# Weight matmuls in runs of one width: hi and lo parts grouped per half block, in a two-layer encoder

## The chip, the cores and the metric

The kernel runs on one core of one Trainium2 chip. The metric is device time in microseconds. The kernel before has a median of 2025.33 us over three runs (2021.2 to 2026.46).

## The reference

What is computed is a two-layer encoder for 256 tokens of width 2048, all in float32:

```python
for l in range(DEPTH):                       # 2 layers
    h = rms_norm(x, norm1_g[l])
    q, k, v, gu, gv = jnp.split(h @ w_in[l], splits, axis=-1)
    ...                                      # windowed attention of 8 heads; spatial gating in chunks of 128
    mixed = jnp.concatenate([rms_norm(attn, attn_out_g[l]), rms_norm(sgu, sgu_out_g[l])], axis=-1)
    x = x + mixed @ w_o[l]
    x = x + conv_gated_ffn(rms_norm(x, norm2_g[l]), w_up[l], conv_w[l], conv_b[l], w_down[l])
```

`conv_gated_ffn` multiplies by `w_up` (2048 x 11264), runs a three-tap convolution over the tokens, gates with silu, and multiplies by `w_down` (5632 x 2048). Nearly all work is in these weight matmuls.

## The kernel before

**Exact parts.** TensorE takes the operands as `fp32r`, a rounded float32. Each weight and each activation is therefore kept as two parts, hi (the rounded value) and lo (the rest), and a product is hi·hi + hi·lo + lo·hi. `split_weights` loads a megabyte of weights into a `raw` tile (L92, SyncE's queue, SP), makes `hi` tiles of 1024 columns on ScalarE (L102) and `lo` tiles on VectorE (L103). There are 3 `raw` buffers and 4 each of `hi` and `lo`. All this is traced as urgent, so the scheduler puts it as early as buffers allow.

**Token-major projections** (`rows_by_cols`, L117 to L119): the activations are the stationary operand, 512 columns of weights stream past, and three 512-wide matmuls in turn make the three products. They compute q, k, v and half of the gating input, at the start of each layer.

**Feature-major projections** (`unit`): 128 x 128 weights are the stationary operand and the 256 tokens stream past. An activation tile holds hi and lo of all tokens side by side (2 x 256 columns). So a hi weight meets all 512 columns (L136, both parts at once), and a lo weight meets the 256 hi columns (L137). One unit makes 256 output features in two PSUM banks, one for each half `i`; it walks over K in blocks of up to 8 groups of 128 rows (`UB`), and each block is one call of `split_weights`: two hi tiles and two lo tiles. `unit` does the gating half of the input projection (w_gu, 4 units in each layer), the output projection (w_o, 8), the up projection (w_up, 44), and the down projection in two parts (w_down, 8 units with 24 groups of K and 8 with 20). That is 2496 hi and 2496 lo matmuls in each layer. `joined` and `residual` then take the result from PSUM.

**Order.** The Tile framework's scheduler sets each engine's order from the traced program, its priorities and the buffers. Within a block, `unit` lists (k, i) with k outside; the unit's last block is sorted so that half 0 is complete before half 1. For each (k, i), hi and lo matmul follow each other.

The lines of attention that come up below: L170 to L172 are the three products of small attention matmuls, L204 broadcasts a per-token factor with the help of ones.

Of the kernel before, what the change touches and what calls it, by code (L numbers as in the profile page):

```python
# [14 lines left out]
P = 128  # L15
D = 2048
SEQ = 256
DEPTH = 2
DFF = 5632
HD = 128  # L20
# [6 lines left out]
KB = 4  # L27
UW = 256
UB = 8
AHEAD = 100000  # L30

# columns of a layer's per-feature parameters, features on partitions
C_N1, C_AG, C_SG, C_N2, C_CW = 0, 16, 24, 32, 48
N_COL = 48 + 4 * 2 * NF
# a layer's row parameters, to be broadcast over partitions
R_QG, R_KG, R_SINK, R_LG, R_LB, R_BS = 0, 128, 256, 264, 264 + 1024, 264 + 2048


# [1 line left out]
def encoder(ctx: ExitStack, tc: tile.TileContext, xT, w_in, w_gu, w_o, w_up, w_down, wsT, pcol, prow, rope, out):  # L40
    nc = tc.nc
# [29 lines left out]
    def mm():  # L71
        return mmp.tile([P, 2, W], F32, tag="mm", name="mm")
# [10 lines left out]
    def urgent():  # L83
        return tc.high_priority(offset=AHEAD)

    # ---- weights: hi and lo parts that add up to the float32 value exactly
    def split_weights(src, step=2 * W):
        n = src.shape[-1]
        with urgent():
            raw = rawp.tile([P, 4 * W], F32, tag="raw", name="raw")  # L90
            if step == 2 * W:
                nc.sync.dma_start(raw[:, :n], src)  # L92
            his, los = [], []
            for h in range(0, n, 2 * W):
                hi = hip.tile([P, 2 * W], F32R, tag="hi", name="hi")
                lo = lop.tile([P, 2 * W], F32R, tag="lo", name="lo")
                for a in range(0, 2 * W, step):
                    part = raw[:, h + a : h + a + step]
                    if step < 2 * W:
                        nc.sync.dma_start(part, src[:, h + a : h + a + step])  # L100
                    cs = slice(a, a + step)
                    nc.scalar.activation(hi[:, cs], part, AF.Copy)  # L102
                    nc.vector.tensor_tensor(out=lo[:, cs], in0=part, in1=hi[:, cs].bitcast(F32), op=ALU.subtract)  # L103
                his.append(hi)
                los.append(lo)
        return his, los

    # tokens x columns: ps[:, m, :] += act(k)[:, m].T @ w(k)
    def rows_by_cols(ps, acts, src, first, last, step=2 * W):
        his, los = split_weights(src, step)  # L110
        for kk in range(KB):
# [6 lines left out]
                nc.tensor.matmul(ps[:, m, :], acts[kk][:, 0, ms], wl, start=False, stop=False)  # L118
                nc.tensor.matmul(ps[:, m, :], acts[kk][:, 1, ms], wh, start=False, stop=s1)  # L119

    # columns x tokens, in two halves: [w.T @ hi + wl.T @ hi | w.T @ lo]
    def unit(acts, w, ps=None, k0=0, k1=None, first=True, last=True):
        ps = mm() if ps is None else ps
        bank = [ps[:, i, :] for i in range(2)] if not isinstance(ps, list) else ps
        k1 = len(acts) if k1 is None else k1
        for b in range(k0, k1, UB):
            n = min(UB, k1 - b)
            his, los = split_weights(w[:, b * UW : (b + n) * UW])
            order = [(k, i) for k in range(b, b + n) for i in range(2)]
            if last and b + n == k1:  # L130
                order.sort(key=lambda v: v[1])
            for k, i in order:
                c = (k - b) % KB * UW + i * P
                wh, wl = (t[(k - b) // KB][:, c : c + P] for t in (his, los))
                s0, s1 = first and k == k0, last and k == k1 - 1
                nc.tensor.matmul(bank[i], wh, acts[k].rearrange("p a b -> p (a b)"), start=s0, stop=False)  # L136
                nc.tensor.matmul(bank[i][:, :SEQ], wl, acts[k][:, 0, :], start=False, stop=s1)  # L137
        return ps

    def joined(ps):  # L140
# [24 lines left out]
        nc.vector.tensor_tensor(out=lo, in0=src, in1=hi.bitcast(F32), op=ALU.subtract)  # L165
        return hi, lo

    # out (+)= a.T @ b from parts
    def matmul3(out, a, b, start=True, stop=True):
        nc.tensor.matmul(out, a[0], b[0], start=start, stop=False)  # L170
        nc.tensor.matmul(out, a[0], b[1], start=False, stop=False)  # L171
        nc.tensor.matmul(out, a[1], b[0], start=False, stop=stop)  # L172

    # squares of feature-major rows, added up block by block
    def add_squares(acc, src, first):
        if first:
            nc.scalar.activation(acc, src, AF.Square)
# [9 lines left out]
        nc.gpsimd.tensor_tensor(out=r, in0=v, in1=mhalf[:, :width], op=ALU.pow)  # L187
        return r

    # 1/rms of every token, tokens on partitions, from squares with features on partitions  # L190
    def inv_rms_cols(acc, n, tag):
        t = tp([P, 2])
        nc.vector.tensor_tensor(out=acc[:, 0, :], in0=acc[:, 0, :], in1=acc[:, 1, :], op=ALU.add)
# [1 line left out]
            nc.tensor.matmul(t[:, m : m + 1], acc[:, 0, m * P : (m + 1) * P], ones[:, :1], start=True, stop=True)  # L195
        return inv_rms(t, n, tag, 2)

    # the same with tokens along the free dimension, on all partitions
    def as_rows(r):
        t = tp([P, SEQ])  # L200
        for m in range(2):
# [4 lines left out]
        nc.scalar.copy(rb, t)  # L206
        return rb

    # ---- loads that every layer needs
    def layer_params(l, eng):  # L210
        pc = lay.tile([P, N_COL], F32, tag="pc", name="pc")
        eng.dma_start(pc[:, :C_CW], pcol[l, :, :C_CW])
        return pc
# [34 lines left out]
                rows.append(t)  # L248
        return ws, rows

    # rotated rows (times the norm's gain): nh heads of [P, nh * HD]
    def rotate(rows, m, nh, tab):
        v = rows.rearrange("p (h d) -> p h d", d=HD)
        a = sl([P, nh, HD])
# [16 lines left out]
        nc.scalar.activation(sq, rows, AF.Square)  # L271
        nc.vector.tensor_reduce(out=ms, in_=sq.rearrange("p (h d) -> p h d", d=HD), axis=AX.X, op=ALU.add)

    # one group's heads, in steps to be traced between the projections' blocks
    def attend(g, ps, r, kT, v, tab, qk, nsink, acc, outs):
        ms = st([P, 2, 4], "qms")
        rot = []
# [74 lines left out]
            outs.append(o)  # L352
        yield

    # feature-major rows times gain and 1/rms, in parts
    def normed(tiles, g0, pc, rb):
        got = []
        for j, t in enumerate(tiles):
# [6 lines left out]
                got.append(split_plain(n))  # L365
        return got

    # ---- start
    with urgent():
        pc = layer_params(0, nc.sync)  # L370
    qk = None
# [1 line left out]
    make_identity(nc, ident)  # L373
    mask = const.tile([P, 2, SEQ], F32, tag="mask", name="mask")
    nc.gpsimd.memset(mask, 0.0)
    # token p sees key 128 + j when j <= p; token 128 + p sees key j when j >= p
    nc.gpsimd.affine_select(
        out=mask[:, 0, P:], in_=mask[:, 0, P:], compare_op=ALU.is_ge, fill=MASKED,
        base=0, pattern=[[-1, P]], channel_multiplier=1,
# [2 lines left out]
        out=mask[:, 1, :P], in_=mask[:, 1, :P], compare_op=ALU.is_ge, fill=MASKED,  # L382
# [25 lines left out]
    for l in range(DEPTH):  # L408
        pc, qk = params
        acts = hT  # L410

        def in_rows(ps, c, b):
            # the very first block comes in smaller pieces
            step = W if (l, c, b) == (0, 2, 0) else 2 * W
            src = w_in[l, c, :, b * KB * W : (b + 1) * KB * W]
            rows_by_cols(ps, acts[b * KB : b * KB + KB], src, b == 0, b == NB - 1, step)

        # keys and values, and the first queries
        psk, psq = mm(), mm()
        for b in range(NB):  # L420
            if l == 0:
# [18 lines left out]
        for m in range(2):  # L440
            t = sl([P, W])
# [6 lines left out]
        for m in range(2):  # L448
            a = rotate(kv[m][:, : 2 * HD], m, 2, tabs[1])
            nc.vector.tensor_tensor(  # L450
                out=a, in0=a, in1=rk[:, 2 * m : 2 * m + 2].unsqueeze(2).to_broadcast([P, 2, HD]), op=ALU.mult
# [21 lines left out]
            it = attend(g, ps, r1, kT, vs, tabs[0], qk, nsink, acca, att)  # L473
            return lambda: next(it)

        # second queries, the first group's attention between them
        first = group_steps(0, psq)
        first()
        ps = chunk(1, [[], [], [turned_keys], [first]])
        second = group_steps(1, ps)  # L480
        second()

        # gates of the spatial part
        vn = []
        stats = st([P, 2, 2, 6], "bns")
        for i in range(2):
            ps = chunk(3 + i, [[[first], [first, second], [first], [second]], [[], [second], [], [second]]][i])
            for m in range(2):
                t = row("vn")
# [43 lines left out]
        for i in range(2):  # L533
            for m in range(2):
                t = vn[2 * i + m]
# [20 lines left out]
        gated(3)  # L556
        gate(3)

        # output projection: the attention half of K first, while the gating half ends
        hT = []  # L560
        accx = lay.tile([P, 2, SEQ], F32, tag="acc", name="acc")
        with urgent():
# [3 lines left out]
        for u in range(8):  # L566
            if u < 3:
                ps = unit(mixT, w_o[l, u], pre[u], NK // 2, NK, first=False)
            else:
                ps = unit(mixT, w_o[l, u])  # L570
# [8 lines left out]
            pc1 = layer_params(l + 1, nc.sync)  # L579
            params = (pc1, layer_params_rest(l + 1, pc1, nc.sync))  # L580

        # gated convolution, features on partitions
        def convolved(ps, ch):
            s = joined(ps)
            nc.vector.tensor_tensor(out=s, in0=s, in1=r2b2[0], op=ALU.mult)  # L585
# [12 lines left out]
        for f0, f1 in ((0, 24), (24, NF)):  # L598
            ys = []
            for f in range(f0, f1, 2):  # L600
                y = sl([P, 2, SEQ])
                ps = unit(acts2, w_up[l, f // 2])
                if f == 0:
                    r2 = inv_rms_cols(accx, D, "y")
                    ps2 = unit(acts2, w_up[l, NF // 2])
                    r2b2.append(as_rows(r2).unsqueeze(1).to_broadcast([P, 2, SEQ]))
                nc.scalar.activation(y, convolved(ps, f), AF.Silu)
                t = convolved(unit(acts2, w_up[l, (NF + f) // 2]) if f else ps2, NF + f)
                nc.vector.tensor_tensor(out=y, in0=y, in1=t, op=ALU.mult)  # L609
                for i in range(2):  # L610
                    ys.append(split_plain(y[:, i, :]))

            # down projection of these features
            last = f1 == NF
            if last and more:
                hT = []
                accx = lay.tile([P, 2, SEQ], F32, tag="acc", name="acc")
            for u in range(8):
                ps = [tp([P, W]) for _ in range(2)] if last and not more and u == 7 else mm()
                unit(ys, w_down[l, u, :, f0 * UW : f1 * UW], ps)  # L620
                if last and not more:
                    for i in range(2):
                        part = ps[i] if isinstance(ps, list) else ps[:, i, :]
                        for a in (0, SEQ):
                            nc.vector.tensor_tensor(out=xs[u][:, i, :], in0=part[:, a : a + SEQ], in1=xs[u][:, i, :], op=ALU.add)
                        nc.sync.dma_start(out[:, 2 * u + i, :], xs[u][:, i, :])
                else:
                    residual(ps, u)
                if last and more:
                    next_rows(u, C_N1, params[0])  # L630
                    add_squares(accx, xs[u], u == 0)
# [56 lines left out]
```

## Time and profile before

| what | us |
|---|---|
| median of 3 runs | 2025.33 (2021.2 to 2026.46) |
| the profiled execution: first to last instruction | 2049.1 |
| TensorE busy (share of the span) | 2036.3 (99%) |
| weight loads busy | 1755.1 (86%) |
| VectorE busy | 1429.4 (70%) |
| ScalarE busy | 1076.5 (53%) |
| weights and the rest moved | 380.26 MB, 186 GB/s |

The profiled execution's own time is known only by its span; what lies around the span is not recorded for it. The table's engine rows are shares of an execution in which engines overlap. Matmuls are pipelined: the record of one reaches into the next, so that a busy TensorE isn't one at its peak, and pace is read from the distance of starts. In the rows that the prediction quotes, "L136 PE MATMUL ... x146: 391/391/391, 229.7 to 280.0" means 146 matmuls of line 136 with their least, median and greatest recorded duration in ns, and the starts of the first and the last in us. A row of the timeline begins with its start and its duration in us. A row of waits reads: who, for whom, us in total, times, longest.

### The profile page before, as it was taken

Reading aid. Unit: us, or ns where it says so; the run is one execution under the profiler, and the core shown is the slowest. Engines: PE = TensorE matmul, PEld = TensorE weight load, DVE = VectorE, ACT = ScalarE, POOL = GpSimd, SP = SyncE. Lnnn points to the kernel's source line nnn. Section 1 sums busy time; section 2 is a strip of 40 time slices with the busy share of each in tenths; the row PEclk is TensorE's granted clock in tenths of the full one; section 3 lists DMA queues with packets and bytes.
Section 4 is the critical chain, followed back from the end, with each engine's and each line's share of the span. In section 5 each row is a group of like instructions: output and inputs, shape, how many; then the busy total and the mean of one; then the engine's idle time right before and its main releaser. Section 6 shows DMA issues by size and latency. Waiting matters only on the chain.

```text
span 2049.1 us, 28253 instructions
## 1 busy us (share of the span) xinstructions
PE 2036.3 (99%) x11320; PEld 1755.1 (86%) x11320; DVE 1429.4 (70%) x1983; ACT 1076.5 (53%) x1427; POOL 19.5 (1%) x25
## 2 busy tenths in 40 slices
PE   8999999999999999999999999999999999999999
PEld 6888888888888888888888888888888888888887
DVE  6878767777745577776567887677777556777754
ACT  6575556555533455554445655555555334555532
POOL 0100000000000000000000000000000000000000
PEclk9999999999999999999999999999999999999999
DMA  8544555555555555555565445555555555555563
GB/s 294 203 149 156 185 190 185 187 188 188 189 186 185 185 185 185 185 186 175 197 224 183 146 147 189 183 189 188 189 187 188 186 185 185 185 185 185 182 209 124
DMA packets 59316, 380.26 MB, mean 186 GB/s; under 512 B 6832, under 2 KB 9648, under 8 KB 15280
## 3 DMA queue, kind: packets, MB, share of 16 engines
q1 hardware_dynamic: 59184, 378.46, 54.9%
q8 instruction: 88, 1.44, 0.3%
q14 instruction: 44, 0.36, 0.1%
HBM read 376.33 MB, written 2.10 MB: 185 GB/s over the span
## 4 chain that ended last, share of the span: by engine, by line
PE 96%; DVE 2%; ACT 0%; DMA 0%; issue 0%; POOL 0%; SPq 0%; ACTq 0%; POOLq 0%
PE mm L136 55%; PE mm L137 28%; PE mm L118 3%; PE mm L119 3%; PE mm L117 3%; DVE lo L103 1%; PE tp L136 0%; DMA raw<-in_w_in 0%; PE tp L342 0%; PE tp L170 0%; PE tp L518 0%; PE tp L172 0%; PE tp L171 0%; ACT hi L102 0%; PE tp L204 0%
## 5 line engine op out<-in xcount | busy, mean ns | idle before, releaser
L136 PE MATMUL mm<-sl,hi 128*128 128x512 f32 x4952 | 1748.6, 398 | 0.0
L137 PE MATMUL mm<-sl,lo 128*128 128x256 f32 x4952 | 1391.0, 281 | 0.0
L103 DVE TENSOR_TENSOR lo<-raw,hi 128x1024 fp32r<-128x1024 f32 (+1 forms) x706 | 861.6, 1221 | 547.5 <-ACT hi L102 542.1
L102 ACT ACTIVATE hi<-raw 128x1024 fp32r<-128x1024 f32 (+1 forms) x706 | 747.7, 1059 | 820.8 <-PE mm L136 626.6
L136 PEld LDWEIGHTS mm<-sl,hi 128*128 128x128 f32 x4952 | 930.1, 188 | 228.4
L137 PEld LDWEIGHTS mm<-sl,lo 128*128 128x128 f32 x4952 | 935.4, 189 | 0.7 <-DVE lo L103 0.3
L117 PE MATMUL mm<-hi,sl 128*128 128x512 f32 x320 | 126.8, 396 | 5.8 <-ACT hi L102 5.8
L118 PE MATMUL mm<-lo,sl 128*128 128x512 f32 x320 | 126.4, 395 | 0.8 <-DVE lo L103 0.8
L119 PE MATMUL mm<-hi,sl 128*128 128x512 f32 x320 | 125.8, 393 | 0.0
L589 ACT ACTIVATE sc<-ev,pc 128x256 f32<-128x256 f32 x176 | 95.2, 590 | 0.2
L593 DVE SCALAR_TENSOR_TENSOR sc<-ev,pc,sc 128x255 f32<-128x255 f32 x176 | 77.1, 479 | 0.1
L590 DVE SCALAR_TENSOR_TENSOR sc<-ev,pc,sc 128x255 f32<-128x255 f32 x176 | 77.0, 478 | 0.0
L117 PEld LDWEIGHTS mm<-hi,sl 128*128 128x128 f32 x320 | 60.7, 190 | 18.3 <-ACT hi L102 6.3
L118 PEld LDWEIGHTS mm<-lo,sl 128*128 128x128 f32 x320 | 60.7, 190 | 13.4 <-DVE lo L103 1.5
L119 PEld LDWEIGHTS mm<-hi,sl 128*128 128x128 f32 x320 | 60.7, 190 | 12.3
L158 ACT ACTIVATE sl<-sl 128x256 fp32r<-128x256 f32 x88 | 32.0, 411 | 72.0 <-DVE sl L609 72.0
L145 DVE TENSOR_TENSOR ev<-mm,ev 128x512 f32<-128x512 f32 x96 | 65.6, 684 | 0.1
L585 DVE TENSOR_TENSOR ev<-ev,rb 128x512 f32<-128x512 f32 x88 | 60.8, 692 | 2.8
L405 DVE TENSOR_TENSOR xs<-mm,xs 128x512 f32<-128x512 f32 x80 | 54.9, 686 | 5.2 <-PE mm L137 5.0
L143 ACT COPY ev<-mm 128x512 f32<-128x512 f32 x96 | 54.6, 569 | 0.0
L159 DVE TENSOR_TENSOR sl<-sl 128x256 fp32r<-128x256 f32 x88 | 33.6, 421 | 18.5 <-ACT sl L158 18.5
L150 ACT ACTIVATE sl<-xs,pc 128x256 fp32r<-128x256 f32 x64 | 29.1, 500 | 15.0 <-DVE xs L405 12.4
(117 smaller groups left out, 620.0 us busy)
## 6 DMA issues: line engine op xcount, KB each, us to landing
raw<-in_w_up SPq DMA_DIRECT2D x176, 1024.0 KB, 5.0
raw<-in_w_down SPq DMA_DIRECT2D x80, 1024.0 KB, 4.8
raw<-in_w_in SPq DMA_DIRECT2D x39, 1024.0 KB, 4.9
raw<-in_w_o SPq DMA_DIRECT2D x32, 1024.0 KB, 5.0
raw<-in_w_gu SPq DMA_DIRECT2D x16, 1024.0 KB, 4.9
raw<-in_w_down SPq DMA_DIRECT2D x16, 512.0 KB, 3.7
sl<-in_prow SPq DMA_DIRECT2D x12, 256.0 KB, 6.4
out_xT<-xs SPq DMA_DIRECT2D x16, 128.0 KB, 1.8
```

The source lines that it names most:

```text
L102: nc.scalar.activation(hi[:, cs], part, AF.Copy)
L103: nc.vector.tensor_tensor(out=lo[:, cs], in0=part, in1=hi[:, cs].bitcast(F32), op=ALU.subtract)
L117: nc.tensor.matmul(ps[:, m, :], acts[kk][:, 0, ms], wh, start=s0, stop=False)
L118: nc.tensor.matmul(ps[:, m, :], acts[kk][:, 0, ms], wl, start=False, stop=False)
L119: nc.tensor.matmul(ps[:, m, :], acts[kk][:, 1, ms], wh, start=False, stop=s1)
L136: nc.tensor.matmul(bank[i], wh, acts[k].rearrange("p a b -> p (a b)"), start=s0, stop=False)
L137: nc.tensor.matmul(bank[i][:, :SEQ], wl, acts[k][:, 0, :], start=False, stop=s1)
L145: nc.vector.tensor_tensor(out=s, in0=ps[:, :, :SEQ], in1=rest, op=ALU.add)
L585: nc.vector.tensor_tensor(out=s, in0=s, in1=r2b2[0], op=ALU.mult)
L589: nc.scalar.activation(t[:, i, :], s[:, i, :], AF.Identity, bias=col(3), scale=col(1))
L590: nc.vector.scalar_tensor_tensor(out=t[:, i, 1:], in0=s[:, i, : SEQ - 1], scalar=col(0), in1=t[:, i, 1:], op0=ALU.mult, op1=ALU.add)
L593: nc.vector.scalar_tensor_tensor(out=t[:, i, : SEQ - 1], in0=s[:, i, 1:], scalar=col(2), in1=t[:, i, : SEQ - 1], op0=ALU.mult, op1=ALU.add)
```

## The change

In `unit`, the block's loop is turned: for each half `i`, first the hi matmuls of all k in the block, then the lo matmuls of all k. The same instructions with the same operands are issued. Halves are now outside in every block, where before they were so in the last block alone.

```diff
-            order = [(k, i) for k in range(b, b + n) for i in range(2)]
-            if last and b + n == k1:
-                order.sort(key=lambda v: v[1])
-            for k, i in order:
-                c = (k - b) % KB * UW + i * P
-                wh, wl = (t[(k - b) // KB][:, c : c + P] for t in (his, los))
-                s0, s1 = first and k == k0, last and k == k1 - 1
-                nc.tensor.matmul(bank[i], wh, acts[k].rearrange("p a b -> p (a b)"), start=s0, stop=False)
-                nc.tensor.matmul(bank[i][:, :SEQ], wl, acts[k][:, 0, :], start=False, stop=s1)
+            for i in range(2):
+                for part in range(2):
+                    for k in range(b, b + n):
+                        c = (k - b) % KB * UW + i * P
+                        w1 = (his, los)[part][(k - b) // KB][:, c : c + P]
+                        if part == 0:
+                            x1 = acts[k].rearrange("p a b -> p (a b)")
+                            nc.tensor.matmul(bank[i], w1, x1, start=first and k == k0, stop=False)
+                        else:
+                            s1 = last and k == k1 - 1
+                            nc.tensor.matmul(bank[i][:, :SEQ], w1, acts[k][:, 0, :], start=False, stop=s1)
```

Three lines are added, so the hi matmul stands at L137 afterwards and the lo matmul at L140; lines further down move by 3.

TensorE before, at the end of an up-projection unit of layer 1: the last hi and lo of its half 0 and the first of its half 1 in the last block (`sl` are activation tiles, one for each k; `hi` and `lo` are weight tiles of four k each; `mm` is the unit's PSUM tile):

```order
L136 MATMUL mm_4014<-sl_2570,hi_4063 128x512
L137 MATMUL mm_4014<-sl_2570,lo_4064 128x256
L136 MATMUL mm_4014<-sl_2573,hi_4063 128x512
L137 MATMUL mm_4014<-sl_2573,lo_4064 128x256
L136 MATMUL mm_4014<-sl_2666,hi_4063 128x512
L137 MATMUL mm_4014<-sl_2666,lo_4064 128x256
L136 MATMUL mm_4014<-sl_2669,hi_4063 128x512
L137 MATMUL mm_4014<-sl_2669,lo_4064 128x256
L136 MATMUL mm_4014<-sl_2378,hi_4059 128x512
L137 MATMUL mm_4014<-sl_2378,lo_4060 128x256
```

And now, the same unit and block, from the second half of the hi run into the lo run:

```order
L137 MATMUL mm_4014<-sl_2570,hi_4063 128x512
L137 MATMUL mm_4014<-sl_2573,hi_4063 128x512
L137 MATMUL mm_4014<-sl_2666,hi_4063 128x512
L137 MATMUL mm_4014<-sl_2669,hi_4063 128x512
L140 MATMUL mm_4014<-sl_2378,lo_4060 128x256
L140 MATMUL mm_4014<-sl_2381,lo_4060 128x256
L140 MATMUL mm_4014<-sl_2474,lo_4060 128x256
L140 MATMUL mm_4014<-sl_2477,lo_4060 128x256
```

A lo tile is first needed a whole hi run after the first hi matmul, and a hi or lo tile is used in two places of the block, once for each half.

ScalarE before, in the up projection of layer 1, from one unit's copy out of PSUM (L143, in `joined`) to the next one's; L102 makes hi tiles, L589 and L607 are the convolution's middle tap and the silu:

```order
L143 COPY ev<-mm 128x512
L102 ACTIVATE hi<-raw 128x1024
L589 ACTIVATE sc<-ev,pc 128x256 x2
L102 ACTIVATE hi<-raw 128x1024
L607 ACTIVATE sl<-sc 128x512
L102 ACTIVATE hi<-raw 128x1024 x2
L143 COPY ev<-mm 128x512
```

And now (L146, L592 and L610 are the same three):

```order
L146 COPY ev<-mm 128x512
L592 ACTIVATE sc<-ev,pc 128x256 x2
L102 ACTIVATE hi<-raw 128x1024 x2
L610 ACTIVATE sl<-sc 128x512
L102 ACTIVATE hi<-raw 128x1024 x2
```

The two hi tiles of a block are now made back to back, because they come free close to each other; the other work stands around the pair. VectorE's lo tiles move likewise. On SP, one load of the token-major projections stands earlier, and in layer 2's down projection six half-size loads, each for the unit after the next, stand behind a unit's second output transfer (L626 before) and no longer ahead of it.

## The prediction

> **What bounds the kernel now.** I read the page's busy shares first, then the granted clock, the chain, the waits of PE, and last the spacing of matmul starts. The page:
>
> ```profile
> PE 2036.3 (99%) x11320; PEld 1755.1 (86%) x11320; DVE 1429.4 (70%) x1983; ACT 1076.5 (53%) x1427; POOL 19.5 (1%) x25
> ...
> PEclk9999999999999999999999999999999999999999
> ...
> PE 96%; DVE 2%; ACT 0%; DMA 0%; issue 0%; POOL 0%; SPq 0%; ACTq 0%; POOLq 0%
> PE mm L136 55%; PE mm L137 28%; PE mm L118 3%; PE mm L119 3%; PE mm L117 3%; DVE lo L103 1%; PE tp L136 0%; DMA raw<-in_w_in 0%; PE tp L342 0%; PE tp L170 0%; PE tp L518 0%; PE tp L172 0%; PE tp L171 0%; ACT hi L102 0%; PE tp L204 0%
> ```
>
> TensorE is busy 99% of the span at full clock, and 83% of the chain is the two lines that the change reorders. The list of waits says that PE hardly waits for anybody; its three longest entries add up to 8 us, and two of them lie in L117 and L118, which the change does not touch:
>
> ```profile
> PE mm L117 <- ACT hi L102: 5.8, 2, 5.4
> PE tp L204 <- DVE sc L203: 1.5, 4, 0.5
> PE mm L118 <- DVE lo L103: 0.8, 1, 0.8
> ```
>
> So the time can only change through the pace at which PE takes matmuls. A matmul's recorded duration overlaps the next one's (398 and 281 ns below are more than the pair takes), so I read the pace from the first and last start of a line in a stretch, with its count. The hi line in three stretches (start columns are the last two numbers before the semicolon):
>
> ```profile
> L136 PE MATMUL mm<-sl,hi x146: 391/391/391, 229.7 to 280.0; 128*128 128x512 f32 x146
> ...
> L136 PE MATMUL mm<-sl,hi x2011: 395/398/403, 309.8 to 1020.0; 128*128 128x512 f32 x183
> ...
> L136 PE MATMUL mm<-sl,hi x1982: 395/398/403, 1330.0 to 2029.9; 128*128 128x512 f32 x199
> ```
>
> One hi and one lo together take 50.3/145 = 346.9 ns in the first stretch, but 710.2/2010 = 353.3 ns and 699.9/1981 = 353.3 ns in the two long ones. The program is the same hi, lo, hi, lo in all three; PE has **two paces** for it, keeps one for hundreds of microseconds, and was in the slow one for 1410 of the 2049.1 us. The last block of each unit already goes column half by column half (hi, lo, hi, lo on one bank) and lies in the same even 353.3 ns, so the order of halves and banks has no price of its own.
>
> **How the timed runs stand to this execution.** The median is 2025.33, which is 23.8 us under the traced span, although a timed run has all of the span's work. PE's waits (8 us) can't hold 23.8 us. If the 3993 pairs of the two long stretches went at 346.9, the span would lose 3993 x 6.4 = 25.6 us and be 2023.5, inside the timed runs' 2021.2 to 2026.46. So I take it that the timed runs mostly have the fast pace already, and that the slow one is a state of this traced execution. This is inference, and the forecast hangs on it.
>
> **The change, part by part.** No instruction is added or removed; 4992 hi and 4992 lo matmuls (40 of each in the last unit write another tile) stand in 608 runs of 8 and 32 runs of 4 of each kind; I count 4992/8 = 624 runs.
>
> *Hi after hi.* The first projection of each layer already sets 512-wide matmuls behind each other, with a new weight load for each:
>
> ```profile
> L117 PE MATMUL mm<-hi,sl x23: 389/389/389, 24.9 to 39.8; 128*128 128x512 f32 x23
> ```
>
> L117, L118 and L119 take turns there, so 22 steps are 66 matmuls: 14.9/66 = 225.8 ns each.
>
> *Lo after lo, and the switches.* The scores of the attention set twelve 256-wide matmuls in a row, and 512-wide ones follow:
>
> ```profile
> 83.63 0.28 PE L170 MATMUL tp<-sl 128*128 128x256 f32 x1
> ...
> 84.94 0.28 PE L172 MATMUL tp<-sl 128*128 128x256 f32 x1
> 85.06 0.40 PE L117 MATMUL mm<-hi,sl 128*128 128x512 f32 x1
> ...
> 86.22 0.39 PE L119 MATMUL mm<-hi,sl 128*128 128x512 f32 x1
> 86.45 0.39 PE L117 MATMUL mm<-hi,sl 128*128 128x512 f32 x1
> ...
> 1111.36 0.40 PE L118 MATMUL mm<-lo,sl 128*128 128x512 f32 x1
> ...
> 1112.52 0.39 PE L117 MATMUL mm<-hi,sl 128*128 128x512 f32 x1
> ```
>
> Twelve from 83.63 to 85.06 are 119 ns each. The first five 512-wide ones behind such a run take 1.16 us both times (85.06 to 86.22, 1111.36 to 1112.52), not 5 x 0.226 = 1.13: PE needs five wide matmuls to find its pace again. A run of 8 hi and 8 lo is then 1.16 + 3 x 0.226 + 8 x 0.119 = 2.79 us. In turn it is 8 x 353.3 = 2.826 us at the slow pace and 8 x 346.9 = 2.775 us at the fast one.
>
> *The sum for a traced execution.* 3993 slow pairs are 499 runs and gain 0.036 us each, 18.0 us; the other 999 pairs, 125 runs, at worst lose 0.015 each, 1.9 us. A trace of the changed kernel should span 2049.1 - 16 = 2033 us.
>
> *The sum for a timed run.* From the fast pace there is nothing to gain. If PE loses 0.03 us behind each lo run there too, it is 624 x 0.015 = 9.4 us (12.5 at 0.02, the rounding of the rows); if that loss belongs to the same disturbed state as the slow pace, it is 0. The second is nearer to the rows: where the slow pace stands, three pairs lose 3 x 6.4 = 19 ns, and a switch loses 15 to 20 ns a run, so the two look like one effect. I take 0, and keep -16 and +12.5 as ends.
>
> A rule bears on this. These rows show a weight load that starts with one matmul, and the matmul that uses it 0.12 us later:
>
> ```profile
> 400.10 0.28 PE L137 MATMUL mm<-sl,lo 128*128 128x256 f32 x1
> 400.10 0.19 PEld L136 LDWEIGHTS mm<-sl,hi 128*128 128x128 f32 x1
> 400.22 0.40 PE L136 MATMUL mm<-sl,hi 128*128 128x512 f32 x1
> ```
>
> The Trainium skill, "TensorE: Matmul & The Clock Gate", section "LDWEIGHTS (loading the stationary operand)", gives a load as its columns over 1.2, which for 128 columns is an estimate of 107 ns, and lets it run under the matmul ahead. By that rule every load fits under either width, one per matmul in both orders, and the sum is 0, against the -16 that the rows give for the trace; the trace agrees that the load is hidden (0.12 us from load to use), and disagrees in that two paces exist at all.
>
> *What supplies PE.* ScalarE makes hi, VectorE makes lo, each for 1024 columns, four buffers of each, three of raw:
>
> ```profile
> L103 DVE TENSOR_TENSOR lo<-raw,hi 128x1024 fp32r<-128x1024 f32 (+1 forms) x706 | 861.6, 1221 | 547.5 <-ACT hi L102 542.1
> L102 ACT ACTIVATE hi<-raw 128x1024 fp32r<-128x1024 f32 (+1 forms) x706 | 747.7, 1059 | 820.8 <-PE mm L136 626.6
> ...
> L137 PEld LDWEIGHTS mm<-sl,lo 128*128 128x128 f32 x4952 | 935.4, 189 | 0.7 <-DVE lo L103 0.3
> ...
> SPq L92 <- DVE lo L103: 1734.9, 336, 12.0
> SPq L626 <- DVE xs L625: 48.3, 10, 10.5
> ...
> raw<-in_w_up SPq DMA_DIRECT2D x176, 1024.0 KB, 5.0
> ```
>
> ScalarE waits 626.6 us for PE to free hi buffers, and SP's queue waits 1734.9 us for raw buffers: the suppliers are ahead. A block is 2 x 2.79 = 5.58 us. Its first hi tile now comes free after 1.84 + 0.95 + 4 x 0.226 = 3.7 us, against 8 x 0.353 = 2.8 before in a block that isn't the unit's last; its first lo tile after 5.1 us, against 2.8. The buffer is wanted two blocks on, its lo at 2 x 5.58 + 1.84 = 13.0, so with 1.06 + 1.22 us for the conversions 5.6 us are left. The second tiles come free at 4.6 and 5.6 us, not later than before, and with them the raw buffer, so loads (5.0 us to land) start no later. The pair of hi conversions that now stands without other work between them (ScalarE's order, above) makes the copy behind it wait at most 1.06 us, with 5.6 us of the next block as cover. In layer 2's last projection SP now issues six half-size loads behind a unit's second output transfer, ahead of it before; the transfer waits for its unit's end (such waits of L626 are 48.3/10 = 4.8 us), and the load is for the unit after the next, 40 pairs of 0.35 us or 14 us on, so that it lands (5.0 us) in time. I cost all this at 0; with the cover gone, a late tile would cost up to 1.2 us (one conversion) a time.
>
> **Rivals.**
> *Faster: timed runs are slow-paced too.* Then 16 us x 2025/2049 are saved: 2009.5. For it: the slow pace fills 69% of the only execution that is seen. Against it: the 23.8 us then have no place.
> *Slower: the switch loss stays.* Timed runs go in turn at 346.9, and each run pair costs 2.79: 2025.3 + 9.4 = 2035, to 2038 at 0.02. It decides, beyond what a measurement can tell (0.3%, 6.1 us), from 9.8 ns a run pair. For it: both switches that I quote show it, one 1028 us after the other. Against it: the likeness to the slow pace.
> *Faster still: lo in a run has a floor under 119 ns in timed runs.* The first step of the lo run is 0.11; seven of eight lo's 7 ns shorter are 7 x 7 x 624 = 31 us: 1994. Nothing shows it for more than one step.
> *Supply turns late.* 1.2 us in every tenth block (31 of 312) are 37 us: 2062. The 5.6 us of slack speak against it.
>
> **How the numbers follow.** No change, 2026 (range of its own 2020 to 2031): 0.40. Faster by the slow pace 0.28, by the floor 0.04. Slower by the switches 0.25, by supply 0.03. So faster 0.32, same 0.40, slower 0.28. The range 2007 to 2038 leaves out the floor, the supply and the edges of the others, less than 0.2.
>
> **What would show it.** In the new trace, hi starts 226 to 234 ns apart and lo starts 119, a run pair at 2.79 us, no stretch at 353.3, a span near 2033, and a gap from span to median of 7 us, not 24: then the forecast's inference holds. A median that falls with the span proves me wrong; so would a gap of hi or lo waits on PE, which would speak for supply.

## The result and the profile after

The changed kernel takes 2036.97 us (median of 20 runs, 2036.45 to 2038.35), the kernel before 2022.76 (20 runs, 2021.02 to 2038.14): ratio 1.0057, 95% interval 1.0044 to 1.0071. It is slower, by 14 us between the medians. The runs of the kernel before fall into groups: here 16 at 2021 to 2026.5 and four at 2034.6 to 2038.1, in the experiments' sessions also some at 2048 to 2051. The changed kernel's runs all lie within 2 us. Each run's list gives its span too, and that of the changed kernel's profiled run is 2035.4 in a time of 2037.18. Span and time thus differ by 1.8 us; with that the kernel before's traced execution (span 2049.1) was a run of about 2050.9 (an estimate), from the slowest group.

The page of the changed kernel, TensorE's pace (hi line, first and last start of each of the two long stretches), the timeline of its matmuls in the first one, merged by line, the three longest waits of PE, and the timeline around the second of them:

```profile
span 2035.4 us, 28177 instructions
...
PE 2020.0 (99%) x11320; PEld 1759.5 (86%) x11320; DVE 1419.4 (70%) x1983; ACT 1037.5 (51%) x1427; POOL 20.4 (1%) x25
...
PEclk9999999999999999999999999999999999999999
```

```profile
L137 PE MATMUL mm<-sl,hi x1978: 387/393/398, 309.6 to 999.9; 128*128 128x512 f32 x198
...
L137 PE MATMUL mm<-sl,hi x1997: 387/393/398, 1319.7 to 2016.7; 128*128 128x512 f32 x200
```

```profile
400.16 1.11 PE L140 MATMUL mm<-sl,lo 128*128 128x256 f32 x8
401.12 2.00 PE L137 MATMUL mm<-sl,hi 128*128 128x512 f32 x8
402.96 1.12 PE L140 MATMUL mm<-sl,lo 128*128 128x256 f32 x8
403.91 2.00 PE L137 MATMUL mm<-sl,hi 128*128 128x512 f32 x8
```

```profile
PE mm L117 <- ACT hi L102: 5.2, 1, 5.2
PE mm L137 <- DVE sl L162: 2.4, 3, 1.1
PE tp L207 <- DVE sc L206: 2.0, 5, 0.5
```

```profile
1216.20 1.12 PE L140 MATMUL mm<-sl,lo 128*128 128x256 f32 x8
1218.41 2.11 PE L137 MATMUL mm<-sl,hi 128*128 128x512 f32 x8 [1.08 <-DVE sl L162]
1220.94 1.67 PE L137 MATMUL mm<-sl,hi 128*128 128x512 f32 x6 [0.42 <-DVE sl L162]
1223.47 0.51 PE L137 MATMUL mm<-sl,hi 128*128 128x512 f32 x1 [0.86 <-DVE sl L162]
```

The pace is now 349.2 ns a pair in both stretches (690.3/1977 and 697.0/1996), between the two paces of the kernel before. In the timeline a hi run takes 402.96 - 401.12 = 1.84 us and a lo run 0.95, so a run pair takes 2.79 us. Over some 580 full run pairs in the trace the mean start-to-start time is 2793.8 ns. In turn at the fast pace (346.67 ns, read from a stretch of 2019 pairs below) it would be 8 x 346.67 = 2773.3. A return from lo to hi therefore costs about 20 ns. It is paid in the hi run: 1.84 us is more than eight hi matmuls at 0.227 us each (1.81), the step with equal widths below, while the lo run at 0.95 is no longer than eight at 0.12, the step in the runs of 32 (3.83/32).

The second row of the waits is new: PE waits for activation tiles (L162, L159 before), all of it near 1217 to 1223 us, in the output projection of layer 2. The list counts idle time alone. From 1216.20 to 1223.47 PE starts 8 lo and 14 hi matmuls, which take 8 x 0.12 + 14 x 0.227 = 4.1 us at the steady steps and took 7.3: the waits cost about 3.1 us there, not 2.4.

### The profile page after: what moved, and what is told of

Same layout as the page of the kernel before. It is cut to its first block, busy times and chain, and to the rows that moved or that the text cites. A ratio compares the mean times of both kernels' runs of the same rounds, so it can differ in the third digit from the quotient of the medians.

```text
span 2035.4 us, 28177 instructions
## 1 busy us (share of the span) xinstructions
PE 2020.0 (99%) x11320; PEld 1759.5 (86%) x11320; DVE 1419.4 (70%) x1983; ACT 1037.5 (51%) x1427; POOL 20.4 (1%) x25
## 5 line engine op out<-in xcount | busy, mean ns | idle before, releaser
L137 PE MATMUL mm<-sl,hi 128*128 128x512 f32 x4952 | 1247.9, 393 | 2.4 <-DVE sl L162 2.4
L103 DVE TENSOR_TENSOR lo<-raw,hi 128x1024 fp32r<-128x1024 f32 (+1 forms) x706 | 844.5, 1218 | 466.4 <-ACT hi L102 380.5
L137 PEld LDWEIGHTS mm<-sl,hi 128*128 128x128 f32 x4952 | 888.9, 189 | 161.8 <-DVE sl L162 4.5
L102 ACT ACTIVATE hi<-raw 128x1024 fp32r<-128x1024 f32 (+1 forms) x706 | 711.7, 1048 | 545.2 <-PE mm L137 401.7
L140 PEld LDWEIGHTS mm<-sl,lo 128*128 128x128 f32 x4952 | 678.1, 190 | 49.6
L140 PE MATMUL mm<-sl,lo 128*128 128x256 f32 x4952 | 694.8, 282 | 0.0
L592 ACT ACTIVATE sc<-ev,pc 128x256 f32<-128x256 f32 x176 | 96.8, 595 | 211.7 <-DVE ev L588 211.7
L593 DVE SCALAR_TENSOR_TENSOR sc<-ev,pc,sc 128x255 f32<-128x255 f32 x176 | 84.5, 481 | 56.6 <-ACT sc L592 56.4
L596 DVE SCALAR_TENSOR_TENSOR sc<-ev,pc,sc 128x255 f32<-128x255 f32 x176 | 85.1, 485 | 6.1
L146 ACT COPY ev<-mm 128x512 f32<-128x512 f32 x96 | 54.6, 568 | 0.6 <-PE mm L140 0.6
L162 DVE TENSOR_TENSOR sl<-sl 128x256 fp32r<-128x256 f32 x88 | 33.6, 422 | 20.4 <-ACT sl L161 20.4
```

What stands on the lines that cost most here:

```text
L137: nc.tensor.matmul(bank[i], w1, x1, start=first and k == k0, stop=False)
L140: nc.tensor.matmul(bank[i][:, :SEQ], w1, acts[k][:, 0, :], start=False, stop=s1)
L592: nc.scalar.activation(t[:, i, :], s[:, i, :], AF.Identity, bias=col(3), scale=col(1))
L593: nc.vector.scalar_tensor_tensor(out=t[:, i, 1:], in0=s[:, i, : SEQ - 1], scalar=col(0), in1=t[:, i, 1:], op0=ALU.mult, op1=ALU.add)
L596: nc.vector.scalar_tensor_tensor(out=t[:, i, : SEQ - 1], in0=s[:, i, 1:], scalar=col(2), in1=t[:, i, : SEQ - 1], op0=ALU.mult, op1=ALU.add)
```

## Experiments

The kernels of one session share a chip and runs of the kernel before; that kernel's runs lie at 2020.7 to 2025.0 (13 runs), 2034.4 to 2038.5 (18) and 2048.2 to 2050.9 (3) in the first session, where one more took 4054.95 for a reason that isn't known; the second has 11, 12 and 6 in such groups, the third 12, 11 and none. I call the first group the fast floor: 2021 to 2025. The lowest run of that kernel is 2020.7 to 2021.0 in every session, which is why times of different sessions are set side by side below. The ratios are to all runs of the kernel before in a session, whose medians were 2034.88, 2036.36 and 2024.74, so they say more of its groups than of an edit; I go by the floor. Diffs of the order are given as loops.

### Runs of 16

```diff
-for i in range(2): for part in range(2): for k in block
+for part in range(2): for i in range(2): for k in block
```

> In each block both halves' hi matmuls come first (16), then both halves' lo matmuls (16): half as many returns from lo to hi (about 320, not 640). Theory A, each return from a lo run to a hi run costs TensorE a fixed 20 to 25 ns and the length of a run costs nothing: 320 returns, 6 to 8 us over the fast floor of 2021, so 2027 to 2029, and 16 hi + 16 lo take 5.57 us in the trace. Rival B, a lo behind a lo costs about 3.6 ns more than a lo behind a hi (that gives the changed kernel's 16 us too, from 7/8 of 4992): 15/16 of them, 17 us, so 2038. Rival C, the changed supply of hi and lo tiles costs the time: about 2037 or more, since tiles are now held longer still.

Measured: 2031.11 us (2030.91 to 2031.36); ratio to the kernel before 0.9981 (0.9956 to 1.0006). Timeline:

```profile
405.17 3.82 PE L139 MATMUL mm<-sl,hi 128*128 128x512 f32 x16
408.82 2.08 PE L141 MATMUL mm<-sl,lo 128*128 128x256 f32 x16
410.74 2.46 PE L139 MATMUL mm<-sl,hi 128*128 128x512 f32 x10
```

A run pair takes 410.74 - 405.17 = 5.57 us, 5567.4 ns on the mean of 277 in the trace, and 16 pairs at the fast pace would be 5546.7: again 20.7 ns a return. Rival B asked for a slower lo run, 2038, and is out. Rival C too, since here tiles are held longest and the time falls. The median is 2 us above theory A's range. PE also waits for activations, as in the changed kernel (L163 is L162 there), but here in the output projection of layer 1, near 207 to 213 us:

```profile
PE mm L139 <- DVE sl L163: 1.5, 3, 0.9
```

These 1.5 us don't fill the 2 us; the rest is open.

### Runs of 4

```diff
-for i in range(2): for part in range(2): for k in block
+for i in range(2): for h in (first 4, last 4 k of the block): for part in range(2): for k in h
```

> Halves outside, and in each half 4 hi, 4 lo, 4 hi, 4 lo: twice the returns (1248). Theory A: 1248 x 17 to 25 ns = 21 to 31 us over 2021, so 2042 to 2052, with four hi behind a lo run at 1.16 - 0.23 = 0.93 us. Rival B: 3/4 of the lo stand behind a lo, 13.6 us, so 2035. Rival C: tiles are released as in the kernel before or earlier, so below 2037.

Measured: 2039.57 us (2039.23 to 2039.77), ratio 1.0034 (1.0009 to 1.0059). Timeline:

```profile
400.84 1.09 PE L139 MATMUL mm<-sl,hi 128*128 128x512 f32 x4
401.76 0.64 PE L141 MATMUL mm<-sl,lo 128*128 128x256 f32 x4
402.24 1.09 PE L139 MATMUL mm<-sl,hi 128*128 128x512 f32 x4
```

1.40 us a run pair, 1403.5 ns over 1223, against 1386.7 at the fast pace: 16.8 ns a return, and 1248 x 16.8 = 21 us. Added to 2021 that makes 2042; the median lies 2.4 us below it, which no row here explains. Rival B's 2035 is out.

### Half by half, hi and lo in turn

```diff
-for i in range(2): for part in range(2): for k in block
+for i in range(2): for k in block: for part in range(2)
```

> Halves outside in every block as in the changed kernel, but hi and lo in turn as before: the one part of the change alone. Theory A and rival B: as the kernel before, 2021 to 2027, at times 13.6 us more when one of the two long stretches takes the slow pace (353.3 ns a pair in place of 346.7). Rival C (order of halves, release of buffers, supply): 2037, as the changed kernel.

Measured: 2024.37 us (2022.26 to 2039.64), eight runs at 2022 to 2025 and four at 2035 to 2040; ratio 0.9977 (0.9943 to 1.0011). The hi line in its profiled run, a run of 2039.3:

```profile
L139 PE MATMUL mm<-sl,hi x2020: 391/391/391, 309.7 to 1009.7; 128*128 128x512 f32 x184
...
L139 PE MATMUL mm<-sl,hi x1952: 395/398/403, 1329.7 to 2019.0; 128*128 128x512 f32 x196
```

The first long stretch took 700.0/2019 = 346.7 ns a pair, the second 689.3/1951 = 353.3. That is one slow stretch in a run of 2039.3, both were slow in the kernel before's traced execution of 2049.1, and traces below with neither slow span 2021 to 2022. So the groups of the kernel before are most likely its two long stretches: none, one or both slow, 2020 x 6.7 ns = 13.5 us each; its own runs near 2021 and 2035 left no trace. And the order of the halves with its other release of buffers costs nothing that these runs show, about 1 us at most; what costs is the runs.

### Runs of 2

```diff
-for i in range(2): for part in range(2): for k in block
+for i in range(2): for k in block: for part in ((0, 1) if k is even else (1, 0))
```

> Halves outside, and hi lo, lo hi, hi lo in turn, so runs of two of each kind: 2496 returns. Theory A, if a return costs the same 20 ns behind two lo as behind eight: 2496 x 20 = 50 us, so 2071. Theory A with a loss that grows with the lo run up to some length: between 2021 and 2071. Rival B: half of the lo stand behind a lo, 9 us, so 2030. Rival C: as the halves alone, 2021 to 2027.

Measured: 2029.28 us (2028.70 to 2029.68), ratio 0.9989 (0.9963 to 1.0014). Timeline:

```profile
399.97 0.62 PE L139 MATMUL mm<-sl,hi 128*128 128x512 f32 x2
400.43 0.40 PE L141 MATMUL mm<-sl,lo 128*128 128x256 f32 x2
400.66 0.63 PE L139 MATMUL mm<-sl,hi 128*128 128x512 f32 x2
...
401.36 0.62 PE L139 MATMUL mm<-sl,hi 128*128 128x512 f32 x2
```

Two run pairs take 1.39 us, 696.8 ns each over 2467, against 693.3: 3.5 ns a return, 2496 x 3.5 = 8.7 us. Rival B's 2030 is hit here, but by accident, since the runs of 16 and of 4 contradict it. A return costs more the more lo matmuls stand ahead of it, from two over four to eight.

### Runs of 32

```diff
-for part in range(2): for i in range(2): for k in block
+turn = (0, 1) in even blocks of K, (1, 0) in odd ones
+for part in turn: for i in range(2): for k in block
```

> As e1_runs16, but every second block of a unit begins with its lo matmuls, so that runs of 32 lo and 32 hi follow each other: about 176 returns. Theory A (20 ns for a return behind eight or more lo, whatever the run's length): 176 x 20 = 3.5 us over 2021, and 3 us of waiting for activations where the attention ends in layer 2, as e1_runs16 had it: 2025 to 2028, without a second or third cluster. Rival: the loss grows on with the lo run (so that 2031 of e1_runs16 stays): 2031.

Measured: 2032.2 us (eleven runs at 2029.88 to 2034.26; the twelfth took 10643.42, for a reason that isn't known), near the 2031 of the rival and 4 us above theory A's range; ratio 0.9986 (0.9952 to 1.0019). But the trace has not the rival's reason:

```profile
410.35 7.44 PE L140 MATMUL mm<-sl,hi 128*128 128x512 f32 x32
417.63 4.00 PE L142 MATMUL mm<-sl,lo 128*128 128x256 f32 x32
421.46 2.91 PE L140 MATMUL mm<-sl,hi 128*128 128x512 f32 x12
...
PE mm L142 <- ACT sl L163: 2.0, 2, 1.0
PE mm L142 <- DVE lo L103: 1.4, 1, 1.4
```

Over 97 run pairs the mean is 11113.3 ns against 11093.3: 20 ns a return, as behind 8 and 16. The loss is full at eight. What is left of the time is waits, and the clock. The odd blocks start with lo matmuls, for which PE waits in the output projections: for a lo tile in layer 1 and for activations in layer 2. (The expectation puts the waits of the runs of 16 in layer 2, too; they were in layer 1.) About the waits in layer 2, TensorE's granted clock falls (PEclk, the third number from the end):

```profile
core 0: us, PE busy (x) PEld busy (x) DVE busy (x) ACT busy (x) POOL busy (x), PEclk, DMA share, GB/s
1200.00:1215.00 15.00, 13.45 (x77) 11.05 (x75) 10.84 (x21) 7.13 (x12) 0.69 (x1) 1.00 0.54 185
1215.00:1225.00 10.00, 8.99 (x32) 7.21 (x33) 5.01 (x11) 2.39 (x5) 0.00 (x0) 0.66 0.31 105
1225.00:1235.00 10.00, 10.00 (x61) 8.87 (x60) 8.78 (x13) 5.96 (x10) 0.00 (x0) 1.00 0.31 107
```

Whether the waits bring it down isn't shown: the changed kernel, too, waits at this place, at a clock of 1.00. At 0.66 of full clock, 10 us lose up to 3.4. With 2021, 3.5 for the returns and 3.4 of waits that makes up to 2031.3. The other runs agree: the one at a mean clock of 1.000 took 2029.88, six at 0.999 took 2031.66 to 2032.25, and four at 0.998 took 2032.22 to 2034.26.

### Lo matmuls as wide as hi

The changed kernel with lo weights streamed against all 512 columns, so it adds the product of the two lo parts.

```diff
-nc.tensor.matmul(bank[i][:, :SEQ], w1, acts[k][:, 0, :], start=False, stop=s1)
+nc.tensor.matmul(bank[i], w1, acts[k].rearrange("p a b -> p (a b)"), start=False, stop=s1)
```

> The changed kernel with lo matmuls 512 columns wide like the hi ones: lo weights also meet the lo activations, 8 hi then 8 lo as before. Theory A, the loss belongs to the change of width (narrow to wide): no loss, 16 matmuls take 16 x 226.7 = 3.627 us, the span is 2035.4 - 12.8 + 4992 x 0.1067 = 2555. Rival: the loss belongs to the change of weight tile from lo to hi: 3.647 us a run pair, 2568.

One run: 2553.37 us, span 2551.6; the expectations were 2555 and 2568. Timeline:

```profile
400.65 1.98 PE L137 MATMUL mm<-sl,hi 128*128 128x512 f32 x8
402.46 1.98 PE L140 MATMUL mm<-sl,lo 128*128 128x512 f32 x8
404.27 1.98 PE L137 MATMUL mm<-sl,hi 128*128 128x512 f32 x8
406.09 1.98 PE L140 MATMUL mm<-sl,lo 128*128 128x512 f32 x8
407.90 0.39 PE L137 MATMUL mm<-sl,hi 128*128 128x512 f32 x1
```

32 matmuls in 7.25 us are 226.6 ns each, and the runs of lo (1.81 us) are as long as those of hi. There is no loss: it belongs to the change from 256 to 512 columns, not to the change of the weights' tile. The span is 3 us below the 2555, which took over the changed kernel's waits for L162: this trace has none.

### One small matmul ahead of a long stretch

The kernel before with one added matmul in each layer, at the start of the up projection's third unit; its result is not read. (The trace shows it as two, 128 x 1 each.)

```diff
+                if mark and (k, i) == (k0, 0):          # unit's first hi; mark=f == 4 in w_up
+                    nc.tensor.matmul(tp([P, 2])[:, :1], ones, ones[:, :1], start=True, stop=True)
                 nc.tensor.matmul(bank[i], wh, acts[k].rearrange("p a b -> p (a b)"), start=s0, stop=False)
```

> The kernel before with one added 128 x 1 float32 matmul in each layer, in the third unit of the up projection, behind a lo and ahead of a hi. Theory D, the pace in turn (346.7 or 353.3 ns a pair) is set by what stood ahead of the stretch and then kept: behind such a matmul in this position the traces so far showed the fast pace four times of four, so all runs lie at 2021 to 2025, and the trace has 346.7 in both long stretches. Rival E, the pace is drawn by chance whatever stands ahead: clusters at 2021, 2035 and 2049 as in the kernel before.

Measured: 2024.09 us, all twelve runs at 2022.67 to 2025.77, against 2036.36 (2020.96 to 2050.55) for the kernel before in that session; ratio 0.9953 (0.9925 to 0.9982). Layer 2, ahead of the added matmul and behind it:

```profile
L138 PE MATMUL mm<-sl,hi x53: 394/398/404, 1309.6 to 1328.0; 128*128 128x512 f32 x53
...
L138 PE MATMUL mm<-sl,hi x1931: 391/394/396, 1334.8 to 2003.9; 128*128 128x512 f32 x194
```

18.4/52 = 353.8 ns a pair ahead of it, 669.1/1930 = 346.7 behind it: the slow pace was there, and from the small matmul on it was gone for the rest of the kernel. Rival E is out for this matmul.

The same matmul moved one place, behind the first hi and ahead of the first lo:

```diff
                 nc.tensor.matmul(bank[i], wh, acts[k].rearrange("p a b -> p (a b)"), start=s0, stop=False)
+                if mark and (k, i) == (k0, 0):
+                    nc.tensor.matmul(tp([P, 2])[:, :1], ones, ones[:, :1], start=True, stop=True)
```

> The same with the added matmul behind a hi and ahead of a lo. Theory D: in the one place where a trace had that, the slow pace followed, so if the position decides, all runs lie near 2049; if only the disturbance decides, 2021 to 2025 like e7_mark_between. Rival E: clusters at 2021, 2035 and 2049.

Measured: 2024.01 us (2021.46 to 2025.31), ratio 0.9929 (0.9898 to 0.9959). So the position does not decide, and the one older place that I had taken for a rule was none. Here the twelve times alone say so: in the profiled run PE went at the fast pace ahead of the added matmul already (49 pairs in 17.0 us in layer 2).

### Back to the changed kernel: the second term

Runs of 8 as in the changed kernel, but the second half of K of the first three output units k by k, in turn.

```diff
+            if not first and k0 == NK // 2:
+                order.sort(key=lambda v: v[0])
```

> The changed kernel, but the second half of K of the first three output-projection units (the gating half, whose activations are made just then) goes k by k in turn as before; all else in runs of 8. Theory A': the changed kernel pays two terms, about 12.8 us for 640 returns and about 3 us because a run of hi matmuls wants all 8 activation tiles at once there (PE waited 2.4 us for L162 in layer 2). So about 3 us less than the changed kernel's 2037: 2034, and no wait of PE for L162's counterpart in the trace. Rival: the waits only move to another place: 2036 to 2037.

Measured: 2034.89 us (2034.37 to 2037.10), ratio 1.0032 (1.0009 to 1.0055), and in the list of waits:

```profile
PE mm L141 <- DVE sl L165: 1.1, 1, 1.1
```

2.1 us less than the changed kernel, where 3 were expected (the two were timed on different chips); one wait of 1.1 us stays, near 1219 us in the output projection of layer 2. The profiled run is one of three at a mean clock of 0.999, which took 2036.41 to 2037.10; in its trace the clock is 0.66 from 15 to 20 us, in the first projection, which the edit doesn't touch. The nine runs at full clock lie at 2034.37 to 2035.30, below the rival's 2036.

### More small matmuls

```diff
-s = joined(unit(acts, w_gu[l, u]))
+s = joined(unit(acts, w_gu[l, u], mark=u == 0))
-ps = unit(mixT, w_o[l, u])
+ps = unit(mixT, w_o[l, u], mark=u == 3)
```

> e7_mark_between with two more such small matmuls in each layer, in the first gating unit and the fourth output unit. Theory D: the slow stretch of the output projection in layer 2 (28 x 9 pairs at 353.3 in e7's trace) turns fast, 1.7 us less where a run had it, about 0.5 us more for the added matmuls: 2022 to 2024, one cluster. Rival: an added matmul draws the pace by chance: runs with one long stretch slow, 2035 and above, appear again.

Measured: 2023.32 us (2022.12 to 2025.48), one cluster, ratio 0.9969 (0.9947 to 0.9991). Against e7_mark_between (2024.09, another session) the gain of 0.8 us is not told apart from none. The trace shows what theory D asks for; the added matmul in the output projection of layer 2 stands at 1227.85 us:

```profile
L138 PE MATMUL mm<-sl,hi x28: 395/398/403, 1218.0 to 1227.5; 128*128 128x512 f32 x28
...
L138 PE MATMUL mm<-sl,hi x134: 392/394/395, 1229.8 to 1275.9; 128*128 128x512 f32 x134
```

Ahead of it 27 pairs took 9.5 us (9.54 by the timeline, 353.3 ns each), behind it 133 took 46.1 (346.6).

## Why the prediction was right or wrong

The time lies inside the range, but the likeliest case, no change at 2026, did not happen. What happened is the second rival, which had a chance of 0.25 and named 2035 to 2038. A range of 31 us holds all three outcomes, so that it held says little.

- **Right in the main: PE's pace is what counts, and it has two values in turn.** A slow stretch is worth 13.5 us (half by half, in turn). Some 3 us of waits come on top, see below.
- **Half right: the timed runs are mostly fast.** That held for the three runs I was shown, where 2023.5 was worked out for the fast pace, and for 16 of the 20. In the three later sessions it held for 36 of 86. The slow pace is no property of a traced execution: timed runs of 2048 to 2051 exist, and the traced one is one of them. What I argued from a gap between span and median was luck of the draw. The sign that I named for it, a new median 7 us from the span on the same side as before, did not come: the median is 1.6 us above the span.
- **Right: the sum for a trace.** 2033 was worked out, 2035.4 came; a run pair of 2.79 us came to the digit, out of the two rows behind the attention's narrow matmuls.
- **Wrong, the step that failed: "the two look like one effect. I take 0".** I set a return's loss to nothing in timed runs because its size (15 to 20 ns) was like what three slow pairs lose (19 ns). The likeness was no reason: the loss is there in each trace of a kernel with runs, and the changed kernel's times have no second group. It is about 20 ns at eight lo and more, 16.8 at four, 3.5 at two. 640 returns (I had 624) x 20 ns = 12.8 us; the 0.015 in the sum was the right term, 0.020 its size.
- **Wrong in a place: "I cost all this at 0" for what supplies PE.** In the changed kernel's `unit` hi and lo tiles were never late, as I said; but I counted weight tiles alone. Activations are made k by k, and a run of hi matmuls wants eight of them within 1.8 us, where in turn took 5.6 us. PE waited 2.4 us for L162 in layer 2, which cost about 3.1. The floor of 2021 + 12.8 + 3.1 makes 2036.9, and 2036.97 was measured.
- **By the Trainium skill's rule** on how long a weight load takes ("TensorE: Matmul & The Clock Gate", section "LDWEIGHTS (loading the stationary operand)"), which I set beside the rows, the order was free and the sum 0; here a return cost 20 ns. The measurement decides.

What makes PE lose these 20 ns, and what separates its two paces inside, stays open: the runs show which orders lose and which matmul restores the pace, not the part of TensorE that does it. The weight loads are not excluded: with equal widths a load has 227 ns until the next one, in a lo run 120.

## What to carry to other kernels

Read TensorE's pace from start to start over long stretches, and compare it between stretches of the same code, before an order of matmuls is changed; one traced execution may stand in a pace that other runs don't have. Narrow matmuls in runs of eight or more, with wide ones behind them, cost about 20 ns here at each return to the wide ones, so group by width only where returns become few, and count the activations, too, that a run wants at once. Where a long even stream of matmuls shows times in groups, one tiny matmul ahead of the stretch may be worth more than a new order: here it brought 2024.09, against 2036.36 for the kernel before in the same session. It gains nothing on that kernel's fast runs; it takes away the slow ones.

## What the runs showed of the hardware

- Alternating 512- and 256-column matmuls, each with a new weight load, ran for some 700 us at 346.7 or at 353.3 ns a pair, at a granted clock of 1.0 in both. A 128 x 1 float32 matmul ahead of or early in the stretches, in either place of the pair, left none of 36 timed runs of three kernels with a slow long stretch (all at 2021 to 2026).
- The loss at a return from 256 to 512 columns, by the length of the lo run, is 3.5 ns (2), 16.8 (4), 20.5 (8), 20.7 (16), 20.0 (32); with equal widths it is none (226.6 ns for each matmul, one run).
- About two waits of 1.0 us in the runs of 32, the granted clock was 0.66 over 10 us (1215 to 1225 us); in the changed kernel it was 1.00 there, with waits of 1.08, 0.42 and 0.86 us.
